# Three pieces of the gates' chain in the linear attention of an encoder block

## The chip, the core and the metric

The kernel runs on one core of one Trainium2 chip. The metric is the device time of one execution in microseconds (us). Three runs of the kernel before took 1631.79, 1632.20 and 1633.09 us; the median is 1632.2 us.

## The reference: what is computed

One layer of an encoder on 1024 tokens with 1024 features. After an RMS norm the input is multiplied by `w_in`, and the columns are split into the queries, keys and values of two attention branches and their gates. Branch A is a gated linear attention with 4 heads, run in both directions:

```python
b = jnp.cumsum(log_g, axis=3)
q_dec = q * jnp.exp(b)
k_inv = k * jnp.exp(-b)
scores = jnp.where(mask, jnp.einsum("bhncd,bhnmd->bhncm", q_dec, k_inv), 0.0)
...
def step(state, inp):
    kv_n, dec_n = inp
    return dec_n[..., None] * state + kv_n, state
...
o_inter = jnp.einsum("bhncd,nbhde->bhnce", q_dec, states)
```

Per chunk of tokens, `b` is the running sum of the log gates; the queries are scaled by exp(b), the keys by exp(-b), and a state (keys by values) goes from one chunk to the next. Branch B is an attention in a window of 128 tokens. Both are gated, added and projected, and a feed-forward part follows.

## The kernel before, in words

All matrix products are float32 products out of float32r parts: each operand is split into a high part, made by ScalarE (ACT), and a low part, made by VectorE (DVE) as the difference, and three matmuls high x high, high x low, low x high are added (`mm3`, lines 76 to 79). TensorE (PE) is handed its instructions in the order in which the program is written (`manual_schedule` for PE). For ACT, DVE and the queue of transfers (SP) a scheduler lays down the order when the program is built: of what it takes for ready it puts first what was written first. On the chip each engine then works through its list in order.

The part around the change is the linear attention: 4 heads with 8 chunks of 128 tokens each, in time slots `t` (lines 597 to 614). Chunks go in pairs. For head `hd` and an even chunk `c`, with n = 8 hd + c:

- `g_gates` (lines 395 to 443) at the head of slot n, an even slot: loads the pair's q and k (`qk`), multiplies the gate codes out (`z`), and makes the gates in one tile `G` (one buffer) by a chain that goes back and forth between ACT and DVE: exponential (L418, ACT), a cap (L419, DVE), logarithm (L420, ACT), running sum (L421, DVE), the chunk ends `sm` (L424, L425), the differences (L428, L429, DVE), two exponentials of `G` (L431 and L432, ACT), the products with k and q (`en` in L434, `G` in L435, DVE), and the splits `kh`, `kl` (L438, L439) and `q2f`, `q2b` (L442, L443).
- `g_scores` (L445) at slot n+3, an odd slot: loads and splits v (`vh`, `vl`), turns `en` round on PE (`kt`, split to `kth`, `ktl`), multiplies the scores, and makes the masked scores `sp` (L470 ACT, L471 DVE), `sh` (L474) and `sl` (L475), the last two on DVE.
- `g_out` (L480) for each chunk at slot n+4: the chunk's keys times values `kv` on PE; the new state `pf` on DVE (L489, or L493 for a head's first chunk); a copy `kb` of the other direction's part (L491, ACT); for the next chunk the decayed state, split to `th` (L501, ACT) and `tl` (L502, DVE); then the output `o` on PE from `sh`, `sl` and from the `th`, `tl` of the chunk before, and its copy `ob` (L509, ACT).
- `g_back_out` (L523) for the other direction, later: adds its product to `ob` (L531, DVE) and moves the backward state one chunk on (`thb` in L520, `tlb` in L521, `kb` in L523).
- `g_turn` (L546): turns a finished chunk round on PE and copies it (`ot`, L552, ACT).

The small products write to a pool of four PSUM banks (`ch`), so a new product waits until an older one's bank has been read by the copy or the addition named above. A second pool of four banks (`mm`) serves the dense projections.

`slot` (L267) writes the stages of a slot in a fixed order, gates, turns, `g_back_out`, `g_out`, `g_scores`, and after each stage an equal share of the slot's dense projection matmuls (34 a slot at first, later 21, 18 and 11, from `GF`). So `g_out` of an even slot comes behind the gates' stage, and that of the odd slot half a slot later comes near the slot's head. The dense matmuls read weights that `wunit` has split two units ahead (`wh` L67, `wl` L69); their results leave by `st` (L138, L141 on DVE, L220 on ACT). DVE also does passes over the input for a later stage (`xn`, L563 and L568).

Of the kernel before, what the change touches and what calls it, by code (L numbers as in the profile page):

```python
# [23 lines left out]
GF = ((8, 34), (24, 21), (36, 18), (1 << 30, 11))  # L24
# [6 lines left out]
def body(tc, i, out):  # L31
    nc = tc.nc
    with ExitStack() as root:
# [8 lines left out]
        def nm(s):  # L42
            uid[0] += 1
            return f"{s}_{uid[0]}"
# [4 lines left out]
        def chtile(shape, dt=F32):  # L49
            return psc.tile(list(shape), dt, tag="ch", name=nm("ch"))  # L50
# [21 lines left out]
        def mm(o, a, b, start, stop):  # L72
            nc.tensor.matmul(o, a, b, start=start, stop=stop)  # L73
# [40 lines left out]
        def put(key, t):  # L114
            d = scratch("_".join(map(str, key)))
            nc.sync.dma_start(out=d, in_=t)
            scr[key] = d
# [139 lines left out]
        def fill(n):  # L257

            while n > 0 and dense:
                try:  # L260
                    next(dense[0])
                    n -= 1
                except StopIteration:
                    dense.pop(0)

        def share(plan, t):
            return next(n for end, n in plan if t < end)  # L267

        def need(key):
            while key not in scr:  # L270
                fill(12)

        def slot(stages, n):

            stages = [f for f in stages if f]
            done = 0
            if not stages:
                fill(n)
            for j, f in enumerate(stages):
                f()  # L280
                t = n * (j + 1) // len(stages)
                fill(t - done)
                done = t
# [106 lines left out]
        def gtile(tag, shape=(P, 256), dt=F32, bufs=2):  # L390
            return gt.tile(list(shape), dt, tag=tag, name=nm(tag), bufs=bufs)
# [4 lines left out]
        gla = {}  # L396

        def g_gates(hd, c):


            pr = Chunk()
            for j in range(2):
                a = gla[hd, c + j] = Chunk()
                a.pr, a.j, a.t = pr, j, slice(j * P, (j + 1) * P)
            s, co = c // 4, (c % 4) * P
            for nme in ("q", "k"):
                need((f"{nme}{hd}", s))
            qk = gtile("qk", (P, 2, 256))
            nc.sync.dma_start(out=qk[:, 0], in_=scr[f"q{hd}", s][:, co:co + 256])
            nc.sync.dma_start(out=qk[:, 1], in_=scr[f"k{hd}", s][:, co:co + 256])  # L410
            z = chtile((P, 2, 256))
            for d in range(2):
                mm(z[:, d], upS[:, d, hd * P:(hd + 1) * P], lrS[:, c * P:(c + 2) * P], True, True)
            G = gtile("G", (P, 4, 2, P), bufs=1)
            Gt = G.rearrange("p a j t -> p a (j t)")
            Gf = G.rearrange("p a j t -> p (a j t)")
            cs, e, csf, ef = G[:, 0:2], G[:, 2:4], Gf[:, 0:512], Gf[:, 512:1024]
            nc.scalar.activation(ef, z.rearrange("p d t -> p (d t)"), AF.Exp, scale=-1.0)  # L418
            nc.vector.tensor_scalar(ef, ef, float(np.expm1(8.0)), None, op0=ALU.min)  # L419
            nc.scalar.activation(ef, ef, AF.Ln, bias=ones[:, 0:1])  # L420
            nc.vector.tensor_tensor_scan(csf, mask.rearrange("p c t -> p (c t)"), ef, 0.0, op0=ALU.mult, op1=ALU.add)  # L421

            pr.sm = gtile("sm", (P, 2, 2, 2), bufs=16)
            nc.vector.tensor_scalar(pr.sm, cs[:, :, :, 63:128:64], -1.0 / 16, None, op0=ALU.mult)  # L424
            nc.vector.tensor_tensor(pr.sm[:, :, :, 1], pr.sm[:, :, :, 1], pr.sm[:, :, :, 0], op=ALU.subtract)  # L425

            late = bass.AP(Gf.tensor, Gf.offset, [list(Gf.ap[0]), [255, 2], [P, 2], [1, P]])
            nc.vector.tensor_tensor(e, late, cs[:, :, :, 63:64].to_broadcast([P, 2, 2, P]), op=ALU.subtract)  # L428
            nc.vector.tensor_scalar(e[:, 1, :, 0:1], cs[:, 1, :, 63:64], -1.0, None, op0=ALU.mult)  # L429

            nc.scalar.activation(csf, ef, AF.Exp, scale=-1.0 / 16)  # L431
            nc.scalar.activation(ef, ef, AF.Exp, scale=1.0 / 16)  # L432
            pr.en = gtile("en", (P, 2, 256))
            nc.vector.tensor_tensor(pr.en, Gt[:, 1:3], qk[:, 1:2].to_broadcast([P, 2, 256]), op=ALU.mult)  # L434
            nc.vector.tensor_tensor(Gt[:, 0:4:3], Gt[:, 0:4:3], qk[:, 0:1].to_broadcast([P, 2, 256]), op=ALU.mult)  # L435
            pr.kh = gtile("kh", (P, 2, 256), FR)
            pr.kl = gtile("kl", (P, 2, 256), FR)
            nc.scalar.activation(pr.kh, pr.en, AF.Copy)  # L438
            nc.vector.tensor_tensor(pr.kl, pr.en, pr.kh.bitcast(F32), op=ALU.subtract)  # L439
            pr.q2 = (gtile("q2f", (P, 2, 256), FR, bufs=3), gtile(f"q2b{c}", (P, 2, 256), FR, bufs=(3, 2, 2, 1)[c // 2]))  # L440
            for q2, x in zip(pr.q2, (Gt[:, 0], Gt[:, 3])):
                nc.scalar.activation(q2[:, 0], x, AF.Copy)  # L442
                nc.vector.tensor_tensor(q2[:, 1], x, q2[:, 0].bitcast(F32), op=ALU.subtract)  # L443
# [116 lines left out]
        def x_norm(k, s):  # L560
            t = xn.tile([P, HT], F32, tag="xn", name=nm("xn"))
            nc.sync.dma_start(out=t, in_=i["xT"][k, s])
            tc.keep_in_program_order(nc.vector.scalar_tensor_tensor(  # L563
                t, t, g1[:, k:k + 1], rstd[:, s * HT:(s + 1) * HT], op0=ALU.mult, op1=ALU.mult))
            return t

        def x_diff(key, k, d, a, b):
            tc.keep_in_program_order(nc.vector.tensor_tensor(d, a, b, op=ALU.subtract))  # L568
            put((key, k), d)

        def x_sums():
            for k in range(KT // 2):
                a = x_norm(k, 0)
                yield
                b = x_norm(k, 1)
                yield
                x_diff("xT1", k, b, b, a)
                yield
                c = x_norm(k + 4, 1)
                put(("x22", k), c)  # L580
                yield
                x_diff("xT2", k, b, c, b)
                yield
                x_diff("xT3", k, a, b, a)
                yield
                c = x_norm(k + 4, 0)
                yield
                x_diff("xT4", k, c, c, b)
                yield
# [4 lines left out]
        qg = load_const(swk, "qg", i["qg"], (P, P))  # L594
        kg = load_const(swk, "kg", i["kg"], (P, P))

        at = {}
        last = 0
        for n in range(NH * NC):
            hd, c = divmod(n, NC)  # L600
            cb = hd * NC + NC + 4 + (NC - 1 - c)
            tt = cb + c % 2 + 2
            for j, (t, f) in enumerate(((n, g_gates), (n + 3, g_scores), (n + 4, g_out),
                                        (cb, g_back_out), (tt, g_turn))):
                if j > 1 or c % 2 == 0:
                    at[t, j + (j == 4 and c % 2)] = (f, hd, c)
                last = max(last, t)
        sums = x_sums()
        with tc.manual_schedule(engines={mybir.EngineType.PE}):
            fill(36)  # L610
            for t in range(last + 1):
                slot([(lambda v=at[t, j]: v[0](*v[1:])) if (t, j) in at else None for j in (0, 5, 4, 3, 2, 1)], share(GF, t))
                if t:
                    next(sums, None)
        glas.close()
# [185 lines left out]
        for n in range(2 * KT):  # L801
            t, g = divmod(n, 2)
# [101 lines left out]
        def pair_T3(f):  # L904
            nme, m, a, b = PAIRS[f]
            g = pend[f]
            product(g.X, wsplit(g.s3, 512), XT["T3"], 4, False, True)
            return result((f"{nme}{m + 4}", 1), g.X, g.p5)
# [69 lines left out]
        with tc.manual_schedule(engines={mybir.EngineType.PE}):  # L978
# [15 lines left out]
            for j in range(0, len(PAIRS), 2):  # L994
# [4 lines left out]
                v = [pair_T3(f) for f in two]  # L999
# [554 lines left out]
```

## Time and profile before

| what | value |
|---|---|
| median of three runs | 1632.2 us (1631.79 to 1633.09) |
| the profiled execution | 1632.87 us; its span, from the first to the last instruction, 1631.1 us |
| granted TensorE clock | 1.00 |
| PE, DVE, ACT busy in the span | 1614.8, 1228.7, 911.6 us |
| slots of the linear attention | from 48.5 us (first L418) to 373 us (last `ot`) |
| gates' chains | 16, the first scan (L421) at 50.95 us, the last at 307.08 us |

How to read it: a row of the timeline gives the start, the duration, the engine, the line, what is written and from what; in brackets stands the idle time of the engine just before and what ended it. Starts of neighbours on one engine lie closer together than durations, since they overlap at their ends. "PE" rows are matmuls, "PEld" the loading of their weights. The list of waits adds up such idle times by the instruction that ended them: total, number, longest.

### The profile page before, as it was taken

To read this page: it belongs to the slowest core of one execution; us is meant where nothing else is said; L and a number is where in the kernel's file an instruction comes from. 1 tells how busy PE (TensorE), PEld (TensorE's weight loads), DVE (VectorE), ACT (ScalarE), POOL (GpSimd) and SP (SyncE) were. 2 spreads that over 40 slices of the span, in tenths; PEclk is the share of its full clock that TensorE was granted. 3 is DMA by queue.
4 is the path that set the end of the run, shared out by engine and by line. 5 is a ranking of instruction groups with operands and counts; after the bars stand their busy time and mean duration, and the time that the engine had idled before them with its cause. 6 is when DMAs were issued, how large, how long until landed. Compare 5 with 4: busy or idle time off the path is not lost.

```text
span 1631.1 us, 23428 instructions
## 1 busy us (share of the span) xinstructions
PE 1614.8 (99%) x7644; PEld 1342.6 (82%) x7644; DVE 1228.7 (75%) x2358; ACT 911.6 (56%) x1867; POOL 0.2 (0%) x4
## 2 busy tenths in 40 slices
PE   9999999999999999999999999999999999999999
PEld 7888888788888888888888888888888888788887
DVE  8568888855989777876955888677777888779655
ACT  7456776873888854544733556754444444354442
POOL 0000000000000000000000000000000000000000
PEclk9999999999999999999999999999999999999999
DMA  8855847788553478777943566643435464695433
GB/s 279 299 171 191 255 152 265 265 268 291 184 165 107 133 253 265 258 239 263 296 123 103 167 201 214 205 142 112 148 111 182 166 221 146 201 331 190 149 97 117
DMA packets 196363, 323.26 MB, mean 198 GB/s; under 512 B 22318, under 2 KB 47790, under 8 KB 196240
## 3 DMA queue, kind: packets, MB, share of 16 engines
q1 hardware_dynamic: 196240, 321.76, 60.4%
q8 instruction: 60, 0.98, 0.3%
q14 instruction: 63, 0.52, 0.1%
HBM read 216.29 MB, written 105.38 MB: 197 GB/s over the span
## 4 chain that ended last, share of the span: by engine, by line
PE 88%; DVE 5%; ACT 4%; DMA 2%; issue 1%; SPq 0%; ACTq 0%; DVEq 0%
PE mm L73 19%; PE mm L856 10%; PE mm L858 10%; PE mm L857 10%; PE mm L1394 7%; PE ch L73 6%; PE ch L1394 6%; PE ch L856 5%; PE ch L858 5%; PE ch L857 5%; PE mm L245 3%; PE ch L762 1%; ACT p L745 1%; DVE G L421 1%; PE ch L712 0%
## 5 line engine op out<-in xcount | busy, mean ns | idle before, releaser
L835 ACT ACTIVATE wh<-ws 128x512 fp32r<-128x512 f32 x164 | 103.0, 630 | 154.1 <-PE mm L857 83.0
L73 PE MATMUL mm<-wh,xh 128*128 128x512 f32 x320 | 127.2, 398 | 1.1 <-ACT st L220 1.1
L73 PE MATMUL mm<-wh,xl 128*128 128x512 f32 x320 | 127.1, 397 | 0.0
L73 PE MATMUL mm<-wl,xh 128*128 128x512 f32 x320 | 126.6, 396 | 0.0
L836 DVE TENSOR_TENSOR wl<-ws,wh 128x512 fp32r<-128x512 f32 x164 | 112.1, 686 | 14.6 <-ACT wh L835 14.2
L67 ACT ACTIVATE wh<-wr 128x512 fp32r<-128x512 f32 x118 | 73.5, 627 | 55.1 <-PE mm L73 21.6
L69 DVE TENSOR_TENSOR wl<-wr,wh 128x512 fp32r<-128x512 f32 x118 | 80.7, 686 | 21.7 <-ACT wh L67 21.3
L835 ACT ACTIVATE wh<-a 128x512 fp32r<-128x512 f32 x66 | 41.7, 632 | 91.1 <-PE ch L1394 42.3
L835 ACT ACTIVATE wh<-wr 128x512 fp32r<-128x512 f32 x76 | 47.9, 631 | 58.9 <-PE mm L857 19.7
L836 DVE TENSOR_TENSOR wl<-a,wh 128x512 fp32r<-128x512 f32 x66 | 45.6, 690 | 41.0 <-ACT wh L835 40.6
L1394 PE MATMUL mm<-hh,wh 128*128 128x512 f32 x176 | 68.6, 390 | 0.6 <-DVE c L1333 0.6
L1394 PE MATMUL mm<-hl,wh 128*128 128x512 f32 x176 | 68.7, 390 | 0.0
L73 PEld LDWEIGHTS mm<-wh,xh 128*128 128x128 f32 x320 | 60.3, 188 | 10.3 <-ACT st L220 1.3
L1394 PE MATMUL mm<-hh,wl 128*128 128x512 f32 x176 | 68.5, 389 | 0.0
L73 PEld LDWEIGHTS mm<-wl,xh 128*128 128x128 f32 x320 | 60.2, 188 | 9.8
L73 PEld LDWEIGHTS mm<-wh,xl 128*128 128x128 f32 x320 | 60.2, 188 | 9.7
L849 DVE TENSOR_TENSOR ws<-wr,wr 128x512 f32<-128x512 f32 x80 | 54.5, 686 | 5.5 <-DMA wr<-in_w_oa_dram 2.5
L836 DVE TENSOR_TENSOR wl<-wr,wh 128x512 fp32r<-128x512 f32 x76 | 51.9, 685 | 7.7 <-ACT wh L835 7.1
L1367 DVE TENSOR_TENSOR hl<-hr,hh 128x512 fp32r<-128x512 f32 x77 | 52.8, 685 | 6.0 <-ACT hh L1366 6.0
L1366 ACT ACTIVATE hh<-hr 128x512 fp32r<-128x512 f32 x77 | 47.6, 618 | 8.9 <-DMA hr<-B 5.0
L1394 PE MATMUL ch<-hh,wh 128*128 128x512 f32 x132 | 51.3, 389 | 0.0
L1394 PE MATMUL ch<-hl,wh 128*128 128x512 f32 x132 | 51.3, 389 | 0.0
(454 smaller groups left out, 4987.1 us busy)
## 6 DMA issues: line engine op xcount, KB each, us to landing
wr<-in_w_fi_dram SPq DMA_DIRECT2D x110, 256.0 KB, 4.0
wr<-in_w_f_dram SPq DMA_DIRECT2D x100, 256.0 KB, 3.7
wh<-wh SPq DMA_DIRECT2D x80, 256.0 KB, 3.3
wl<-wl SPq DMA_DIRECT2D x80, 256.0 KB, 3.0
B<-c SPq DMA_DIRECT2D x44, 256.0 KB, 2.1
T<-st SPq DMA_DIRECT2D x44, 256.0 KB, 2.9
a<-in_w_fo_dram SPq DMA_DIRECT2D x44, 256.0 KB, 5.3
hr<-T SPq DMA_DIRECT2D x44, 256.0 KB, 2.6
```

The lines of the kernel that those rows point to most:

```text
L67: nc.scalar.activation(h, raw, AF.Copy)
L69: nc.vector.tensor_tensor(l, raw, h.bitcast(F32), op=ALU.subtract)
L73: nc.tensor.matmul(o, a, b, start=start, stop=stop)
L245: nc.tensor.matmul(Y[q], w[:, c], x, start=f0, stop=f1, skip_group_check=True)
L835: nc.scalar.activation(h, src, AF.Copy)
L836: nc.vector.tensor_tensor(l, src, h.bitcast(F32), op=ALU.subtract)
L849: nc.vector.tensor_tensor(t, x, y, op=op)
L856: nc.tensor.matmul(o, h[:, c], x[kk][0], start=start and kk == 0, stop=False, skip_group_check=True)
L857: nc.tensor.matmul(o, h[:, c], x[kk][1], start=False, stop=False, skip_group_check=True)
L858: nc.tensor.matmul(o, l[:, c], x[kk][0], start=False, stop=kk == nk - 1, skip_group_check=True)
L1367: nc.vector.tensor_tensor(l, r, h.bitcast(F32), op=ALU.subtract)
L1394: nc.tensor.matmul(ys[m], a[:, c], b, start=f0, stop=f1, skip_group_check=True)
```

## The change

`g_gates` is cut into three functions, called at three places. What stays in `g_gates`, at the head of slot n: the loads of `qk`, the matmuls `z`, and the chain up to the chunk ends `sm` (L425). `g_decays` is called in the same slot n, right behind its last stage (`g_out`, once there are outputs) and ahead of that stage's dense matmuls: the differences, the two exponentials and the products with k and q. `g_parts` is called in the odd slot n+1, right behind its last stage (`g_scores`): the splits `kh`, `kl`, `q2f`, `q2b`. No instruction is added or taken away, and none gets another shape; the matmuls on PE, and which dense matmuls stand between them, are the same ones in the same order. Tiles keep their numbers of buffers. In slots that had no stage before, the piece is the only stage and the dense matmuls follow it.

```diff
             nc.vector.tensor_tensor(pr.sm[:, :, :, 1], pr.sm[:, :, :, 1], pr.sm[:, :, :, 0], op=ALU.subtract)
 
+            pr.qk, pr.G = qk, G
+
+        def g_decays(hd, c):
+            pr = gla[hd, c].pr
+            qk, G = pr.qk, pr.G
+            Gt = G.rearrange("p a j t -> p a (j t)")
+            Gf = G.rearrange("p a j t -> p (a j t)")
+            cs, e, csf, ef = G[:, 0:2], G[:, 2:4], Gf[:, 0:512], Gf[:, 512:1024]
             late = bass.AP(Gf.tensor, Gf.offset, [list(Gf.ap[0]), [255, 2], [P, 2], [1, P]])
             nc.vector.tensor_tensor(e, late, cs[:, :, :, 63:64].to_broadcast([P, 2, 2, P]), op=ALU.subtract)
...
             nc.vector.tensor_tensor(Gt[:, 0:4:3], Gt[:, 0:4:3], qk[:, 0:1].to_broadcast([P, 2, 256]), op=ALU.mult)
+
+        def g_parts(hd, c):
+            pr = gla[hd, c].pr
+            Gt = pr.G.rearrange("p a j t -> p a (j t)")
             pr.kh = gtile("kh", (P, 2, 256), FR)
...
-        at = {}
+        at, behind = {}, {}
...
+            if c % 2 == 0:
+                behind[n] = (g_decays, hd, c)
+                behind[n + 1] = (g_parts, hd, c)
...
-                slot([(lambda v=at[t, j]: v[0](*v[1:])) if (t, j) in at else None for j in (0, 5, 4, 3, 2, 1)], share(GF, t))
+                work = [[at[t, j]] for j in (0, 5, 4, 3, 2, 1) if (t, j) in at]
+                if t in behind:
+                    work = work or [[]]
+                    work[-1].append(behind[t])
+                slot([lambda v=v: [f(*a) for f, *a in v] for v in work], share(GF, t))
```

What the scheduler made of it differs in the order of neighbours on ACT, DVE and SP. Below are three places; the lines of the changed kernel are 8 higher from L428 to L435 of before, 12 higher up to the slots, and 19 higher in the attention that follows them.

**Slot 8** (head 1's first pair of chunks; `pf`, `th`, `tl` belong to the output of head 0's chunk 4). On ACT before, from the copy of an output to `kh`:

```order
L509 COPY ob_253_1482<-ch_1475 128x256
L431 ACTIVATE G_1417<-G_1417 128x512
L491 COPY kb_248_1467<-ch_1458 128x256
L432 ACTIVATE G_1417<-G_1417 128x512
L501 ACTIVATE th_1471<-pf_1465,dec_1469 128x256
L498 ACTIVATE dec_1509<-sm_1191,sm_971 128x1
L438 ACTIVATE kh_1432<-en_1429 128x512
```

The same place on ACT in the changed kernel, where the two exponentials are L439 and L440:

```order
L521 COPY ob_248_1465<-ch_1458 128x256
L503 COPY kb_243_1450<-ch_1441 128x256
L513 ACTIVATE th_1454<-pf_1448,dec_1452 128x256
L439 ACTIVATE G_1417<-G_1417 128x512
L510 ACTIVATE dec_1499<-sm_1191,sm_971 128x1
L440 ACTIVATE G_1417<-G_1417 128x512
L450 ACTIVATE kh_1580<-en_1471 128x512
```

`kb` and `th` have moved ahead of the two exponentials. On DVE before:

```order
L489 SCALAR_TENSOR_TENSOR pf_1465<-pf_1303,dec_1307,ch_1458 128x256
L429 TENSOR_SCALAR G_1417<-G_1417 128x2
L434 TENSOR_TENSOR en_1429<-G_1417,qk_1411 128x512
L435 TENSOR_TENSOR G_1417<-G_1417,qk_1411 128x2x256
L502 SCALAR_TENSOR_TENSOR tl_1472<-pf_1465,dec_1469,th_1471 128x256
L439 TENSOR_TENSOR kl_1433<-en_1429,kh_1432 128x512
```

And on DVE in the changed kernel:

```order
L501 SCALAR_TENSOR_TENSOR pf_1448<-pf_1293,dec_1297,ch_1441 128x256
L437 TENSOR_SCALAR G_1417<-G_1417 128x2
L514 SCALAR_TENSOR_TENSOR tl_1455<-pf_1448,dec_1452,th_1454 128x256
L442 TENSOR_TENSOR en_1471<-G_1417,qk_1411 128x512
L443 TENSOR_TENSOR G_1417<-G_1417,qk_1411 128x2x256
L580 TENSOR_TENSOR xn_1408<-xn_1408,xn_854 128x512
```

`tl` has moved ahead of the two products, and `kl` has gone further back.

**Slot 20** (the third pair of head 2). On ACT before, from the logarithm to the copy of a turned chunk, with two results of a projection (`st`) between:

```order
L420 ACTIVATE G_2765<-G_2765,ones 128x512
L220 ACTIVATE st_2815<-mm_2326,rstdt 128x512
L67 ACTIVATE wh_2988<-wr_2986 128x512
L501 ACTIVATE th_2833<-pf_2829,dec_2831 128x256
L431 ACTIVATE G_2765<-G_2765 128x512
L220 ACTIVATE st_2846<-mm_2327,rstdt 128x512
L432 ACTIVATE G_2765<-G_2765 128x512
L552 COPY ot_2870<-ch_2867 128x256
```

In the changed kernel:

```order
L420 ACTIVATE G_2765<-G_2765,ones 128x512
L220 ACTIVATE st_2798<-mm_2309,rstdt 128x512
L67 ACTIVATE wh_2988<-wr_2986 128x512
L220 ACTIVATE st_2836<-mm_2310,rstdt 128x512
L513 ACTIVATE th_2816<-pf_2812,dec_2814 128x256
L439 ACTIVATE G_2765<-G_2765 128x512
L564 COPY ot_2860<-ch_2857 128x256
L440 ACTIVATE G_2765<-G_2765 128x512
```

The second `st` has moved ahead of `th`, and `ot` ahead of the second exponential.

**Slots 22 and 23** (the end of head 2's gates). On DVE before, from `tl` to the addition `ob` of the other direction:

```order
L502 SCALAR_TENSOR_TENSOR tl_3071<-pf_3064,dec_3068,th_3070 128x256
L439 TENSOR_TENSOR kl_3019<-en_3015,kh_3018 128x512
L443 TENSOR_TENSOR q2f_3022<-G_3003,q2f_3022 128x256
L443 TENSOR_TENSOR q2b_646_3023<-G_3003,q2b_646_3023 128x256
L568 TENSOR_TENSOR xn_2526<-xn_2625,xn_2526 128x512
L138 SCALAR_TENSOR_TENSOR st_3102<-mm_2849,rstd 128x512
L138 SCALAR_TENSOR_TENSOR st_3106<-mm_2850,rstd 128x512
L531 TENSOR_TENSOR ob_478_2381<-ob_478_2381,ch_3135 128x256
```

In the changed kernel:

```order
L514 SCALAR_TENSOR_TENSOR tl_3054<-pf_3047,dec_3051,th_3053 128x256
L580 TENSOR_TENSOR xn_2526<-xn_2615,xn_2526 128x512
L138 SCALAR_TENSOR_TENSOR st_3092<-mm_2839,rstd 128x512
L138 SCALAR_TENSOR_TENSOR st_3096<-mm_2840,rstd 128x512
L451 TENSOR_TENSOR kl_3220<-en_3070,kh_3219 128x512
L543 TENSOR_TENSOR ob_473_2364<-ob_473_2364,ch_3125 128x256
L455 TENSOR_TENSOR q2f_3223<-G_3003,q2f_3223 128x256
L455 TENSOR_TENSOR q2b_697_3224<-G_3003,q2b_697_3224 128x256
```

The pass over the input, the two results `st` and the addition `ob` have moved ahead of the splits `q2f` and `q2b`.

## The prediction

> **What bounds the kernel now.** I read the page's busy times first, then PE's waits in the linear attention, then four windows, then the timeline around the waits. The page's first part:
>
> ```profile
> PE 1614.8 (99%) x7644; PEld 1342.6 (82%) x7644; DVE 1228.7 (75%) x2358; ACT 911.6 (56%) x1867; POOL 0.2 (0%) x4
> ```
>
> PE is busy in 99% of the span. The change puts nothing else on PE and leaves PE's order alone, so it can win only time in which PE waits, and only where the change reaches: the slots, from 45 to 345 us. PE's waits there, all of them (total, number, longest):
>
> ```profile
> PE ch L73 <- DVE tl L502: 1.6, 3, 0.9
> PE ch L73 <- ACT ot L552: 1.1, 2, 0.9
> PE mm L73 <- ACT st L220: 1.1, 1, 1.1
> PE ch L73 <- DVE ob L531: 0.6, 2, 0.4
> PE ch L73 <- ACT th L501: 0.3, 1, 0.3
> PE ch L73 <- DVE sl L475: 0.3, 1, 0.3
> PE ch L73 <- DVE sh L474: 0.3, 1, 0.3
> ```
>
> That is 5.3 us in 11 waits. Three windows hold them; the window 250 to 278 has none. Columns: busy time of PE, PEld, DVE, ACT and POOL, the granted clock, the DMA share, GB/s:
>
> ```profile
> 125.00:151.00 26.00, 24.42 (x143) 20.98 (x142) 22.01 (x48) 16.48 (x41) 0.00 (x0) 1.00 0.57 183
> 222.00:250.00 28.00, 26.48 (x154) 22.01 (x153) 23.98 (x58) 21.07 (x60) 0.00 (x0) 1.00 0.56 187
> 250.00:278.00 28.00, 28.00 (x159) 24.21 (x158) 22.51 (x50) 16.43 (x45) 0.00 (x0) 1.00 0.85 282
> 278.00:322.00 44.00, 41.78 (x246) 35.36 (x245) 38.95 (x92) 36.96 (x104) 0.00 (x0) 1.00 0.74 247
> ```
>
> PE's gaps are 1.58, 1.52 and 2.22, 5.3 again, at a clock of 1.00 everywhere. But a wait costs more than its bracket. Two of them on PE's timeline:
>
> ```profile
> 144.22 0.28 PE L73 MATMUL ch<-vl,sh 128*128 128x256 f32 x1
> 144.34 0.28 PE L73 MATMUL ch<-vh,sl 128*128 128x256 f32 x1
> 144.95 0.39 PE L73 MATMUL ch<-th,q2f 128*128 128x256 f32 x1 [0.34 <-ACT th L501]
> 146.28 0.38 PE L73 MATMUL ch<-tl,q2f 128*128 128x256 f32 x1 [0.94 <-DVE tl L502]
> ```
>
> Undisturbed neighbours start 0.12 apart (144.22, 144.34); here the steps are 0.61 and 1.33, so 0.49 + 1.21 = 1.70 is lost where the brackets say 1.28: 0.21 more for each restart. Eleven waits make the pool 5.3 + 11 x 0.21 = 7.6 us. That is all the change can remove.
>
> The Trainium skill (Perfetto Trace Analysis, Identifying the Most-Contended Engine) says that matmul busy time is a poor measure of PE's headroom, since pipelined matmuls look smaller, and that the busy share of LDWEIGHTS is a good one. By that rule the three windows, held against the quiet one, miss 98 x 24.21/28.00 - 78.35 = 6.4 us of loading, or 7.4 us of time. The trace agrees: the starts give 7.6, the busy time 5.3. By the busy time alone the sum below would be about -2.5.
>
> **The change part by part.** *The second piece, L428 to L435, behind the outputs.* Slot 8 on ACT and DVE:
>
> ```profile
> 126.70 0.63 ACT L431 ACTIVATE G<-G 128x512 f32<-128x512 f32 x1 [0.42 <-DVE G L429]
> 127.24 0.35 ACT L491 COPY kb<-ch 128x256 f32<-128x256 f32 x1
> 127.49 0.63 ACT L432 ACTIVATE G<-G 128x512 f32<-128x512 f32 x1
> 128.03 0.50 ACT L501 ACTIVATE th<-pf,dec 128x256 fp32r<-128x256 f32 x1
> ```
>
> ```profile
> 128.16 0.69 DVE L434 TENSOR_TENSOR en<-G,qk 128x512 f32<-128x512 f32 x1 [1.55 <-ACT G L432]
> 128.77 0.68 DVE L435 TENSOR_TENSOR G<-G,qk 128x512 f32<-128x512 f32 x1
> 129.37 0.48 DVE L502 SCALAR_TENSOR_TENSOR tl<-pf,dec,th 128x256 fp32r<-128x256 f32 x1
> ```
>
> In the changed order `th` stands ahead of both exponentials, 0.54 + 0.54 = 1.08 us of ACT (starts 126.70 to 127.24 and 127.49 to 128.03), and `tl` ahead of `en` and `G`, 129.37 - 128.16 = 1.21 of DVE. DVE's wait of 1.55 for the exponential no longer lies ahead of `tl` either. The waits on record for `th` and `tl` are 0.3 (one) and 1.6 (three), all behind an even slot's gates. (a) **All four go: 1.9 + 4 x 0.21 = 2.7.** The largest, 0.49 + 1.21, is covered because both steps come forward there.
>
> *Outputs that wait in ACT's row.* Slot 20 on ACT:
>
> ```profile
> 223.82 0.62 ACT L431 ACTIVATE G<-G 128x512 f32<-128x512 f32 x1
> 224.34 0.67 ACT L220 ACTIVATE st<-mm,rstdt 128x512 f32<-128x512 f32 x1
> 224.91 0.62 ACT L432 ACTIVATE G<-G 128x512 f32<-128x512 f32 x1
> 225.43 0.36 ACT L552 COPY ot<-ch 128x256 f32<-128x256 f32 x1
> ```
>
> PE waited 0.9 for this `ot`; the exponential that `ot` passes is worth 225.43 - 224.91 = 0.52; the second `st` and `th` still stand ahead of it. Of the pool's `ot` 1.1, `st` 1.1 and `ob` 0.6 (2.8 in five waits, 3.9 with restarts) I take about half: 0.7 of `ot`, 0.3 of `st`, since its bank waits behind a full row, and all 0.6 of `ob` with its restarts, 0.4. (b) **2.0 go**, with bounds of 0 and 3.9.
>
> *The third piece, L438 to L443, a slot later.* Slots 22 and 23 on DVE:
>
> ```profile
> 242.45 0.68 DVE L439 TENSOR_TENSOR kl<-en,kh 128x512 fp32r<-128x512 f32 x1
> 243.05 0.42 DVE L443 TENSOR_TENSOR q2f<-G,q2f 128x256 fp32r<-128x256 f32 x1
> 243.38 0.42 DVE L443 TENSOR_TENSOR q2b<-G,q2b 128x256 fp32r<-128x256 f32 x1
> 243.72 0.69 DVE L568 TENSOR_TENSOR xn<-xn,xn 128x512 f32<-128x512 f32 x1
> 244.32 1.28 DVE L138 SCALAR_TENSOR_TENSOR st<-mm,rstd 128x512 f32<-128x512 f32 x2
> 245.52 0.41 DVE L531 TENSOR_TENSOR ob<-ob,ch 128x256 f32<-128x256 f32 x1
> ```
>
> The three splits hold DVE from 242.45 to 243.72, 1.27 us. `q2f` and `q2b` now come behind `ob`, 0.67 of it, more than the longest `ob` wait of 0.4: that is why I let `ob` go. `kl`, `q2f` and `q2b` themselves are read from slot n+3 on, over a slot after their new place, so their lateness costs PE nothing; without that cover it would be their 1.27 a pair. `G` has one buffer, so the next pair's first exponential must wait for `q2b`; between the two lies the rest of an odd slot.
>
> (c) The waits for `sh` and `sl` (0.6, 1.0 with restarts) stay: both stand on DVE ahead of the third piece's new place, and nothing ahead of them is taken away.
>
> (d) **What comes in their place: 1.1.** Work that was ready early now fills the holes: the order puts passes `xn` (0.69 each) ahead of `sl` in some odd slots, and one `sl` has a slack of only 0.24 (rows in the last rival). 0.69 - 0.24 + 0.21 = 0.66 there at most, 0 if DVE was idle before it; I take 0.6, near the upper end, since DVE's row nearest to it (242.45 to 245.52 above) has no gap. And in 278 to 322 DVE works 38.95 of 44.00, so PE, coming earlier, meets it late once more: 0.5, between 0 and the 2.2 that the window loses now.
>
> No wait is added. `th`, which waits for `pf`, now stands ahead of the exponentials on ACT, so those, `en` and `G` wait behind it; PE reads what becomes of them three slots on. SP's loads of `qk` stay at the slot's head, and none of PE's waits above was for a transfer.
>
> Sum: -2.7 - 2.0 + 1.1 = **-3.6**. Against the profiled execution, 1632.87, that is 1629.3; it lies 0.7 above the median, 1632.2, from which it gives **1628.6**.
>
> **The rivals.** *Everything goes.* PE's eleven waits are all of one kind, something late by up to 1.2 us, and the pieces free 1.08 on ACT and 1.21 + 1.27 on DVE per pair. Then -7.6: 1624.6. Against it: `sh` and `sl` are passed by nothing. Chance 0.13.
>
> *Given back.* In the last window DVE is 89% busy, and in 222 to 250 it is 86%. If DVE's own work sets the pace there, only the burst at 125 to 151 is won, 0.46 + 1.70 = 2.2 with its three restarts (the first is the 0.3 for `tl` that is left of the 1.6 and 0.3), less 1.0 of new waits as in (d): 1631.0. Chance 0.17.
>
> *Too few banks.* The waits for `ot`, `ob` and `st` are for four `ch` and four `mm` banks in rotation; if they only move along, (a) alone is won, less (d): -1.6, 1630.6. The Trainium skill (Perfetto Trace Analysis, Optimization Strategy) says that consistent bubbles can mean too little SBUF or PSUM for the next tile; here five of eleven waits are of that kind, but not in a steady beat, which speaks against it. Chance 0.11.
>
> *Slower: the pieces fall ahead of the scores.* `en` and `G` (1.21) and the splits (1.27) now compete in DVE's row with `sh` and `sl`, which come in the odd slots, where the gates had been done long before. Two `sl` on DVE, and their readers on PE with a third place:
>
> ```profile
> 218.78 0.42 DVE L475 TENSOR_TENSOR sl<-sp,sh 128x256 fp32r<-128x256 f32 x1
> 235.06 0.42 DVE L475 TENSOR_TENSOR sl<-sp,sh 128x256 fp32r<-128x256 f32 x1
> ```
>
> ```profile
> 219.44 0.28 PE L73 MATMUL ch<-vh,sl 128*128 128x256 f32 x1
> 236.51 0.28 PE L73 MATMUL ch<-vh,sl 128*128 128x256 f32 x1
> 320.63 0.28 PE L73 MATMUL ch<-vl,sh 128*128 128x256 f32 x1
> 320.96 0.39 PE L73 MATMUL ch<-vh,sl 128*128 128x256 f32 x1
> ```
>
> Slacks: 219.44 - 219.20 = 0.24, 236.51 - 235.48 = 1.03, none at 320.96 (a step of 0.33 where 0.12 is usual), and none where the 0.3 for `sl` is on record. A delay d costs 4d - 1.27 + 2 x 0.21 there. With both pieces, d = 2.48, that is 9.1; against the 4.7 of (a) and (b) the kernel loses 4.4: 1636.6. It is slower than before from d = 1.4, by over 0.2% from d = 2.2. For it: little slack. Against it: in the order the splits are written behind the scores, and the scheduler takes what was written first. Chance 0.15.
>
> **How the numbers follow.** The forecast has 0.44, with a range of its own from 1627.0 ((d) nothing, (b) a little more) to 1630.3 ((b) 0.3). 0.2% is 3.3 us, about what a measurement of this kernel can tell from no change: 1628.9. Of the forecast 0.30 lies below, 0.14 above. Faster: 0.30 + 0.13 + 0.02 from the middle cases = 0.45; same: 0.14 + 0.26 = 0.40; slower: 0.15. The range reaches from 1624.6 to 1633.5, where (d) takes its upper bounds, 0.66 + 2.2, against the 2.2 of the first burst alone (1632.9), and half the spread of the three runs, (1633.09 - 1631.79) / 2 = 0.65, is added; outside lie the slower case and a little below.
>
> **What would show it.** Right: PE's list of waits has no `th` or `tl` any more, `ob` gone, `ot` and `st` shorter, `sh` and `sl` still there and perhaps longer; PE's gaps in the windows 125 to 151 and 222 to 250 under 0.5 us each. Wrong: new waits for `sl`, `sh` or `ktl` in odd slots of a us or more, waits for `kl` or `q2f`, a DVE over 95% busy around 278 to 322, or a difference that arises outside 45 to 345 us.

## The result and the profile after

The changed kernel takes 1629.11 us (median of 11 runs, 1627.65 to 1631.99); the kernel before, run beside it, 1632.95 us (11 runs, 1631.32 to 1634.92). The ratio is 0.9978, with a 95% interval of 0.9971 to 0.9986: 3.6 us less, between 2.3 and 4.7. The forecast was 3.6 less. As a sum it held; of its four terms (d) was far too small, and what the other terms and some uncounted small hold-ups gave beyond the forecast made up for it.

PE's waits of the changed kernel from 45 to 345 us (total, number, longest; L141, L220, L564 and L486 are `st` on DVE, `st` on ACT, `ot` and `sh`):

```profile
PE mm L73 <- DVE st L141: 1.8, 1, 1.8
PE mm L73 <- ACT st L220: 1.0, 1, 1.0
PE ch L73 <- ACT ot L564: 0.2, 1, 0.2
PE ch L73 <- DVE sh L486: 0.2, 1, 0.2
```

The waits for `th`, `tl` and `ob` are gone, and of those for `ot` only 0.2 is left. But the longest wait of the list is a new one, for a result `st` on DVE, and the old one for an `st` on ACT has hardly changed. The windows of before, and one more:

```profile
125.00:151.00 26.00, 25.22 (x147) 21.69 (x145) 22.51 (x49) 16.47 (x42) 0.00 (x0) 1.00 0.53 177
152.00:156.00 4.00, 3.96 (x12) 3.19 (x13) 3.18 (x7) 1.71 (x3) 0.00 (x0) 0.59 0.70 266
222.00:250.00 28.00, 28.00 (x167) 24.36 (x166) 24.86 (x61) 21.57 (x61) 0.00 (x0) 1.00 0.58 191
278.00:322.00 44.00, 42.45 (x253) 36.36 (x252) 39.52 (x94) 36.44 (x104) 0.00 (x0) 1.00 0.79 263
```

From 222 to 250 PE no longer waits at all. The 0.78 that is missing from 125 to 151 is the first part of one wait, which ends at 152. In the 4 us from 152 on, the granted clock is 0.59. Here is that place on PE:

```profile
149.60 0.39 PE L73 MATMUL mm<-wl,xh 128*128 128x512 f32 x1
149.82 0.40 PE L73 MATMUL mm<-wh,xl 128*128 128x512 f32 x1
152.04 0.50 PE L73 MATMUL mm<-wh,xh 128*128 128x512 f32 x1 [1.82 <-DVE st L141]
152.38 0.40 PE L73 MATMUL mm<-wl,xh 128*128 128x512 f32 x1
...
153.36 0.63 PE L73 MATMUL mm<-wh,xh 128*128 128x512 f32 x1
153.79 0.63 PE L73 MATMUL mm<-wl,xh 128*128 128x512 f32 x1
```

The step across the wait is 2.22 where 0.23 is usual, so 1.99 is lost; then steps of 0.43 follow until 156.

Since PE's matmuls come in the same order in both kernels, the start of one and the same matmul in the two traces tells how far ahead the changed kernel is. Four matmuls serve as marks; they start at 48.03, 168.02, 252.20 and 346.14 in the kernel before, and at 47.69, 168.95, 250.40 and 342.83 in the changed one. So the changed kernel is 0.34 ahead at the first mark, 0.93 behind at the second, 1.80 ahead at the third and 3.31 at the last. By stretches: **1.27 lost in the first, 2.73 won in the second, 1.51 won in the third**, 2.97 won in all. The 0.34 at the start and some 1.3 after the last mark lie outside the stretch from 45 to 345; they differ from one execution to the next (0.24 and 0.4 in e1 below, which is the same kernel). The same marks are used for every experiment.

### The profile page after: what moved, and what is told of

Its sections match the earlier page's. It is cut to its first block, busy times and chain, and to the rows that moved or that the text cites. A ratio compares the mean times of both kernels' runs of the same rounds, so it can differ in the third digit from the quotient of the medians.

```text
span 1626.5 us, 23425 instructions
## 1 busy us (share of the span) xinstructions
PE 1613.5 (99%) x7644; PEld 1343.2 (83%) x7644; DVE 1227.7 (75%) x2358; ACT 911.5 (56%) x1867; POOL 0.2 (0%) x4
## 4 chain that ended last, share of the span: by engine, by line
PE 90%; DVE 4%; ACT 4%; DMA 2%; issue 1%; SPq 0%; ACTq 0%; DVEq 0%
PE mm L73 19%; PE mm L875 10%; PE mm L877 10%; PE mm L876 10%; PE mm L1413 7%; PE ch L73 7%; PE ch L1413 6%; PE ch L876 5%; PE ch L875 5%; PE ch L877 5%; PE mm L245 3%; PE ch L781 1%; ACT p L764 1%; ACT xh L323 1%; ACT sq L330 0%
```

## The experiments

Theory A, from the prediction: the gain is the state parts `th` and `tl` coming ahead of the exponentials and products (second piece). Rival B: the third piece brings it, by freeing DVE. About the loss in the first stretch, theory A says that the time won at 130 and 146 was given back at 152, where DVE's row sets when `st` comes; rival C says that DVE sets the pace all over this stretch, so that any wait taken away comes back nearby.

**e1, the changed kernel again.** No edit.

> The changed kernel once more, as a yardstick for the others. If the new wait of 1.8 us for the output st (L141) at 152 us comes from the order on DVE, it stands in this profile too, between 1.7 and 1.9; if it was an accident of one execution, it is gone or under 1. The lower granted clock behind it (0.59 from 152 to 156) may come or not: if the wait alone sets it off it comes again. Ratio to before 0.9970 to 0.9986.

Ratio 0.9979 (0.9970 to 0.9988). The wait for `st` is there again (1.9), the marks give +1.40, -2.70 and -1.52 (minus is won). The pattern belongs to the program.

**e2, the second piece alone; e3, the third piece alone.** In e2 both lines of the table `behind` become one, and the slot appends both functions; in e3 the second piece goes back to the slot's head:

```diff
-                behind[n] = (g_decays, hd, c)
-                behind[n + 1] = (g_parts, hd, c)
+                behind[n] = ((g_decays, hd, c), (g_parts, hd, c))     # e2
+                at[n, 0] = (lambda *v: (g_gates(*v), g_decays(*v)), hd, c)     # e3
+                behind[n + 1] = (g_parts, hd, c)                               # e3
```

> Only the second piece moved (L428 to L435 of before behind the outputs); the splits follow it directly. Theory A (the gain is the state parts th and tl coming ahead of the exponentials and products): the waits for th and tl are gone, the ob waits (0.6) stay because the splits again stand ahead of ob, and the wait for st at 152 stays: 2 to 3 us faster than before, ratio 0.9980 to 0.9990. Rival B (the third piece frees DVE and brings the gain): within 1 us of before, waits for tl still 1 us or more.

> Only the third piece moved (the splits kh, kl, q2f, q2b into the odd slot); the exponentials and products stay at the slot's head. Theory A: the waits for th and tl stay (1.5 to 2 us), those for ob go (0.6 and their restarts, 1.0), no wait for st at 152, since PE does not come earlier there: 0.5 to 1.5 us faster, ratio 0.9990 to 0.9997. Rival B: 3 us or more faster.

e2: ratio 1.0003 (0.9994 to 1.0011); marks -0.24, -0.50, -0.36. e3: ratio 0.9978 (0.9969 to 0.9988); marks -0.56, -1.93, -1.56, in all 4.05 won. PE's waits in e2 and then in e3 (lists of waits from 45 to 345):

```profile
PE mm L73 <- DVE st L141: 1.9, 1, 1.9
PE ch L73 <- DVE sh L486: 1.2, 2, 0.9
PE ch L73 <- DVE ob L543: 1.1, 2, 0.6
PE mm L73 <- ACT st L220: 0.4, 1, 0.4
PE ch L73 <- ACT ob L521: 0.3, 1, 0.3
PE ch L73 <- DVE sl L487: 0.3, 2, 0.2
```

```profile
PE mm L73 <- ACT st L220: 1.7, 1, 1.7
PE ch L73 <- DVE tl L514: 1.0, 2, 0.6
PE ch L73 <- ACT ob L521: 0.4, 1, 0.4
```

In the lists each piece does to its own waits roughly what theory A said: the second takes all for `th` and `tl` and leaves 1.1 for `ob` on DVE (at 230 and 314, though, where the kernel before had 229 and 246); the third takes those for `ob` on DVE and leaves 1.0 for `tl`, less than the 1.5 to 2 expected, and none for `th`. But their worth is the other way round. The second piece gives back at 152 what it won, and the third alone is as fast as both. Theory A falls as an account of where the time went; B holds for the total. That freed time on DVE is how the third piece does it, these two runs do not show.

**e4, more room at 152.** The `st` of 152 us and a second one right behind it on DVE each free one of the four `mm` banks for the next projection (v1, first half), whose first unit goes through its four tiles in turn, three matmuls each. e4 takes the first two units by pairs of tiles, so PE has 12 matmuls to do ahead of the freed banks instead of 6:

```diff
                         us.append(next_unit())
-                        if k < KT - 2:
+                        if (name, s) == ("v1", 0) and k < 2:
+                            if k:
+                                for t2 in (0, 2):
+                                    for k2 in range(2):
+                                        for t in (t2, t2 + 1):
+                                            yield from unit_mm(k2, t)
+                        elif k < KT - 2:
                             for t in range(4):
                                 yield from unit_mm(k, t)
```

> The changed kernel, with the first two units of one projection (v1, first half) taken by pairs of banks, so that PE needs the two banks that the st of 152 us frees 6 matmuls (1.4 us) later. Theory A (the 2.2 us won at 130 and 146 are given back at 152, where DVE's closed row sets when st comes): the wait there falls from 1.8 to under 0.5 and PE is 1.4 to 2 us ahead of the changed kernel behind it, up to 3.5 where the clock also stays at 1.00: ratio to before 0.9960 to 0.9970. Rival C (DVE sets the pace in all of this stretch): as much wait turns up at the next places within 20 us, and the ratio stays near 0.9978.

Ratio 0.9971 (0.9960 to 0.9983); 1627.67 us (6 runs) where e1, on the same chip, took 1629.2. (Part of this is the clock: 5 of e1's 11 executions show a mean clock below 1.000, none of e4's.) No wait at 152, the clock at 1.00, and marks of -2.25, -1.44 and -1.52: 5.21 won. `st` on DVE in e4, and PE's 12th and 13th matmul of the projection:

```profile
150.78 0.68 DVE L141 TENSOR_TENSOR st<-mm,rstd 128x512 f32<-128x512 f32 x1
```

```profile
151.39 0.40 PE L73 MATMUL mm<-wh,xl 128*128 128x512 f32 x1
151.63 0.40 PE L73 MATMUL mm<-wh,xh 128*128 128x512 f32 x1
```

`st` ends at 151.46, only 0.17 ahead of the 13th matmul. In the first stretch C is refuted: what was won is kept. In the second it has a point, since 1.3 less is won there than by the changed kernel.

**e5, fewer steps ahead of `st`.** Updates `kb` of the backward state stood in DVE's row ahead of `st`, two of them written later in the program than that `st`:

```diff
-                    nc.vector.scalar_tensor_tensor(a.kb, n.kb, dec[:, 0:1], a.kb, op0=ALU.mult, op1=ALU.add)
+                    tc.keep_in_program_order(nc.vector.scalar_tensor_tensor(a.kb, n.kb, dec[:, 0:1], a.kb, op0=ALU.mult, op1=ALU.add))
```

> The changed kernel, with each update of the backward state kb (L523 of before) kept behind what was written before it on DVE. In the row ahead of the st at 152 two of the four kb (149.99 to 151.0) drop out; the step ktl ahead of them cannot come earlier, since it waits for kth on ACT until 149.4. If DVE's closed row sets when st comes, st starts about 1.0 earlier and PE's wait falls from 1.8 to between 0.5 and 1.1; ratio to before 0.9970 to 0.9978. If DVE is simply too slow for this whole stretch, the kb updates are missed later and as much wait turns up within 20 us.

Ratio 0.9975 (0.9965 to 0.9985), marks -0.79, -2.47, -1.25. The changed kernel's DVE row up to `st`:

```profile
147.44 0.48 DVE L533 SCALAR_TENSOR_TENSOR tlb<-kb,decb,thb 128x256 fp32r<-128x256 f32 x1
147.84 1.00 DVE L535 SCALAR_TENSOR_TENSOR kb<-kb,decb,kb 128x256 f32<-128x256 f32 x2
148.90 0.48 DVE L533 SCALAR_TENSOR_TENSOR tlb<-kb,decb,thb 128x256 fp32r<-128x256 f32 x1
149.38 0.69 DVE L475 TENSOR_TENSOR ktl<-ch,kth 128x512 fp32r<-128x512 f32 x1
149.99 1.06 DVE L535 SCALAR_TENSOR_TENSOR kb<-kb,decb,kb 128x256 f32<-128x256 f32 x2
150.97 0.43 DVE L483 COPY_PREDICATED sp<-tri,ch 128x256 f32<-128x256 uint32 x1
151.30 0.68 DVE L141 TENSOR_TENSOR st<-mm,rstd 128x512 f32<-128x512 f32 x1
```

And e5's:

```profile
148.23 0.48 DVE L535 SCALAR_TENSOR_TENSOR kb<-kb,decb,kb 128x256 f32<-128x256 f32 x1
149.29 0.48 DVE L533 SCALAR_TENSOR_TENSOR tlb<-kb,decb,thb 128x256 fp32r<-128x256 f32 x1 [0.58 <-ACT thb L532]
149.69 0.48 DVE L535 SCALAR_TENSOR_TENSOR kb<-kb,decb,kb 128x256 f32<-128x256 f32 x1
150.09 0.68 DVE L475 TENSOR_TENSOR ktl<-ch,kth 128x512 fp32r<-128x512 f32 x1
150.85 0.45 DVE L483 COPY_PREDICATED sp<-tri,ch 128x256 f32<-128x256 uint32 x1
151.19 0.68 DVE L141 TENSOR_TENSOR st<-mm,rstd 128x512 f32<-128x512 f32 x1
```

The wait fell from 1.8 to 1.3; 0.5 to 1.1 was expected to be left. Seen from the first mark (0.38 later in this execution), `st` comes 0.49 earlier: two `kb` are out of the row, but `tlb` now waits 0.58 for `thb` on ACT and holds the row. So `st`'s time is set by what stands ahead of it on DVE, waits included. Within the next 20 us no new wait turned up; one of 0.65 for `sh` is new at 316.

**e6, the kernel before with such a bank order; e7, the changed kernel with it; e8, the third piece alone with it.** The condition of e4 is widened to all these projections but v0:

```diff
-                        if (name, s) == ("v1", 0) and k < 2:
+                        if name != "v0" and k < 2:
```

> The kernel before, with the first two units of each such projection (all but v0) taken by pairs of banks. If the bank order only gives room where PE comes too early, the kernel before gains little by it: no wait at 153 was there, the st wait at 295 (1.05, with its restart 1.2) goes, those for th, tl, ob and ot stay: 0.5 to 1.5 us faster, ratio 0.9990 to 0.9997. If the bank order is a gain by itself, 3 us or more, ratio under 0.9982.

> The changed kernel with the same bank order in all these projections. Both st waits (1.8 at 152, 1.0 at 293) fall under 0.3: 2.5 to 4 us less than the changed kernel in the slots, ratio to before 0.9955 to 0.9968. If the waits only move on, the ratio is that of the run with one projection reordered, 0.9971, or worse.

> As e7, with the third piece alone moved. If the second piece is worth the waits for tl and th at 130 and 146 and this was hidden only by the wait at 152, this kernel shows those waits again (1.0 and restarts) and is 1 to 2 us slower than e7. If the third piece alone brings the gain, it is within 0.5 us of e7.

e6: 0.9993 (0.9984 to 1.0002), marks -0.84, -0.40, -0.02. e7: 0.9967 (0.9955 to 0.9980), marks -1.65, -1.41, -2.05. e8: 0.9967 (0.9955 to 0.9980), marks -1.12, -1.90, -2.30. The bank order is little by itself. In e7 the `st` wait at 293 is gone, but a wait of 1.1 for the output copy `ob`, on ACT as well, stands at 292 in its place (in e6 too, 1.2), and by the marks e7, 5.11 ahead in all, is no further than e4 with one projection reordered. The second piece adds nothing to the third here: e7 is 0.5 ahead of e8 in the first stretch and loses it in the second; by time they lie within the 0.5 us that had been set for this, though e8 still has 0.7 of waits for `tl`.

**e9, one reason for the end of the `ot` wait.** In the kernel before, a pass over the input (`xn`, 0.68) stood on DVE between `sl` and the cap of the next gates' chain (L419):

```profile
219.12 0.68 DVE L568 TENSOR_TENSOR xn<-xn,xn 128x512 f32<-128x512 f32 x1
219.72 0.42 DVE L419 TENSOR_SCALAR G<-G 128x512 f32<-128x512 f32 x1
```

In the changed kernel and in e3 the cap stands right behind `sl`, at 219.20 and 219.11, and the chain came sooner. e9 moves that pass, and the one of slot 27, in the kernel before:

```diff
+                if t in (19, 27):
+                    next(sums, None)
                 slot([(lambda v=at[t, j]: v[0](*v[1:])) if (t, j) in at else None for j in (0, 5, 4, 3, 2, 1)], share(GF, t))
-                if t:
+                if t and t not in (19, 27):
                     next(sums, None)
```

> The kernel before, with the passes over the input of slots 19 and 27 written ahead of the slot's stages instead of behind them, so that on DVE no pass (0.68) stands between sl and the cap of the next gates' chain at 219. Theory E: what the third piece won at 226 is this pass, which went forward into the room that the splits left. Then the chain on ACT and DVE comes 0.6 earlier, ot with it, and PE's wait for ot (0.9) falls under 0.4; the waits for ob at 229 and 246 and those for tl and th stay: 0.5 to 1 us faster in the slots, ratio 0.9993 to 0.9999. Rival: the room on ACT (kh, q2f, q2b) brings ot forward; then the wait for ot stays at 0.7 or more.

Ratio 0.9998 (0.9989 to 1.0007), marks -0.22, -0.81, +0.28. PE's first waits in the second stretch:

```profile
224.83 0.38 PE L73 MATMUL ch<-vh,kth 128*128 128x256 f32 x1 [0.45 <-ACT ot L552]
226.78 0.39 PE L73 MATMUL ch<-vh,sh 128*128 128x256 f32 x1 [0.98 <-ACT ob L509]
```

The wait for `ot` halves, from 0.89 to 0.45, between the two expectations. But the output's copy `ob` now waits on ACT behind `q2f` and `q2b`:

```profile
225.76 0.40 ACT L442 ACTIVATE q2f<-G 128x256 fp32r<-128x256 f32 x1
226.07 0.40 ACT L442 ACTIVATE q2b<-G 128x256 fp32r<-128x256 f32 x1
226.38 0.35 ACT L509 COPY ob<-ch 128x256 f32<-128x256 f32 x1
```

So the pass explains about half of the `ot` wait, and what it wins is lost again at once behind the splits on ACT; in e3, where the splits are out of the way too, the wait for `ot` is gone and that for `ob` on ACT is 0.37. The 0.81 of this stretch comes later, from 240 to 246: there the `ob` wait of 0.44 goes, against the expectation, although the splits still stand ahead of that `ob` on DVE. DVE's chain comes 1.5 earlier there, seen from the first mark.

**e10, a wait that was to be longer.** As e4, but with the other pair of tiles first:

```diff
-                                for t2 in (0, 2):
+                                for t2 in (2, 0):
```

> The changed kernel, with the first two units of the projection v1 (first half) begun with the two banks that the st of 152 us frees, so that PE needs them 6 matmuls (1.4 us) earlier. If DVE's row sets when st comes, st stands at the same time as in the changed kernel (about 151.3) and PE's wait grows from 1.8 to 3.2; PE is 1.4 us later behind it. If a long wait is what brings the lower granted clock, it comes here for certain (under 0.65 in the 4 us behind the wait). Ratio to before 0.9980 to 0.9996. If PE's own coming sets st's time, the wait stays near 1.8.

No wait came at 152; ratio 0.9971 (0.9960 to 0.9982), marks -2.31, -1.42, -1.55, as in e4. `st` starts at 150.92, and PE does the projection's first 12 matmuls from 148.78 on without a wait; so the pair that is now first has the free banks. The program appears to give the banks out in order of first use, and the edit did not make what it was meant to. It serves as a second run of e4 and tells nothing on longer waits.

**e11, the second piece alone with e4's bank order; e12, the third alone with it.** The edits are those of e2 and e3 above, each on top of e4's.

> The second piece alone, with the one projection (v1, first half) started by pairs of banks as in e4. If the second piece is worth the waits for th and tl at 130 and 146 as soon as there is room at 152, PE keeps 2.0 to 2.4 us of the first burst, and the slots give about 3 us in all: ratio to before 0.9980 to 0.9987. If the second piece is worth nothing even with that room, the ratio is 0.9993 to 1.0003, and the waits turn up elsewhere.

> The third piece alone, with the same one projection started by pairs of banks. Its own wait at 152 was only 0.2, so the bank order should bring it under 0.4 us: ratio 0.9970 to 0.9978, with the waits for tl (1.0 and restarts) still there, and 1 us slower than e4 if the second piece is worth those waits; the same as e4 (0.9971) and no wait for tl if it is worth nothing.

e11: 0.9982 (0.9973 to 0.9991), marks -2.41, -0.28, -0.36. e12: 0.9973 (0.9963 to 0.9983), marks -1.16, -1.88, -1.58. With room at 152 the second piece keeps its 2.4 us of the first stretch, which it had lost in e2. On top of the third piece it is worth 1.1 there (e4 against e12, 2.25 and 1.16), less 0.4 in the second stretch; by the times, 0.9971 and 0.9973, the two cannot be told apart.

The marks by piece, with minus for won:

| kernel | 48 to 168 | 168 to 252 | 252 to 346 | sum | ratio |
|---|---|---|---|---|---|
| changed | +1.27 | -2.73 | -1.51 | -2.97 | 0.9978 |
| e2, second piece | -0.24 | -0.50 | -0.36 | -1.10 | 1.0003 |
| e3, third piece | -0.56 | -1.93 | -1.56 | -4.05 | 0.9978 |
| e11, second, room at 152 | -2.41 | -0.28 | -0.36 | -3.05 | 0.9982 |
| e12, third, room at 152 | -1.16 | -1.88 | -1.58 | -4.62 | 0.9973 |
| e4, both, room at 152 | -2.25 | -1.44 | -1.52 | -5.21 | 0.9971 |

e4, e7, e8, e10 and e12 took 1627.1 to 1627.7 us and are below both the kernel before and, by about 1.5 us, the changed one (on the same chip in e4 alone); which of them is best cannot be told apart.

## Why the prediction was right, and which of its steps were not

- **The pool** (7.6 us, and nothing outside the slots): held. The most that any kernel here wins in the slots is 5.3 (e8).
- **(a), `th` and `tl` go, 2.7:** the waits went, and the size was right: 2.41 of it, in the first stretch, is what e11 keeps. But in the changed kernel nothing of these 2.41 is left, because of (d); only the `tl` wait at 313, 0.6 with its restart, stays won.
- **(b), half of 3.9:** the total, 2.0, is about what came (`ot` 1.4 to 0.4 and `ob` 1.1 to nothing with restarts, `st` unchanged: 2.1). For `ob` the step named, the splits moved behind it, is enough, since both waits go in e3; it is not the only way, since the wait at 246 falls to 0.10 in e2 and to nothing in e9 with the splits still ahead. For `ot` the step named failed: passing the exponential was not needed, since e3 loses the wait with both exponentials still ahead of `ot`; a pass `xn` that went forward is half of it (e9). ACT in e3:

```profile
224.13 0.62 ACT L440 ACTIVATE G<-G 128x512 f32<-128x512 f32 x1
224.65 0.67 ACT L220 ACTIVATE st<-mm,rstdt 128x512 f32<-128x512 f32 x1
225.22 0.36 ACT L564 COPY ot<-ch 128x256 f32<-128x256 f32 x1
```

For `st` at 295 the reason given, "its bank waits behind a full row", was wrong: the row was not full. ACT in the kernel before, where that `st` follows at 295.10, and then in the changed kernel:

```profile
293.65 0.63 ACT L431 ACTIVATE G<-G 128x512 f32<-128x512 f32 x1 [1.60 <-DVE G L429]
```

```profile
291.39 0.51 ACT L513 ACTIVATE th<-pf,dec 128x256 fp32r<-128x256 f32 x1 [1.41 <-DVE pf L505]
291.80 0.62 ACT L439 ACTIVATE G<-G 128x512 f32<-128x512 f32 x1
292.32 0.67 ACT L220 ACTIVATE st<-mm,rstdt 128x512 f32<-128x512 f32 x1
```

ACT stood idle for 1.60 while the exponential at its head waited for `G` from DVE; now it stands idle for 1.41 while `th` waits for `pf`, and `st` is queued behind in both. The prediction had named this queue ("`th`, which waits for `pf`, now stands ahead") but only for the exponentials.

- **(c), `sh` and `sl` stay:** mostly held. By the steps between matmuls 0.9 was lost to them before and 0.6 is left, 0.3 for `sl` at its old place and 0.35 for `sh` at 317.
- **(d), 1.1 given back in odd slots and in 278 to 322:** this step failed, in place and in size. Where it was put, hardly anything came: the gaps in 278 to 322 fell from 2.22 to 1.55. Instead 1.99 came at 152, for a tile of which the prediction does not speak, and 1.7 more behind it. The trace of before had shown the place. The end of that `st` and the first matmul into its bank, in the kernel before:

```profile
151.84 0.68 DVE L141 TENSOR_TENSOR st<-mm,rstd 128x512 f32<-128x512 f32 x1
```

```profile
152.79 0.39 PE L73 MATMUL mm<-wh,xh 128*128 128x512 f32 x1
```

`st` ended at 152.52, 0.27 ahead of its reader, behind a DVE row without a gap from 146. In the changed kernel PE's matmul just ahead of it starts at 149.82 instead of 152.56, 2.74 earlier, and `st` ends at 151.98, 0.54 earlier; 2.74 - 0.54 - 0.27 = 1.93, and 1.99 came. From the trace of before alone, the 2.2 that the prediction itself won at 125 to 151, less the slack of 0.27, gives 1.9 for a `st` that stays where it is: that could have been priced. The 1.7 lost behind the wait is 0.1 at the restart and the rest the lower clock in this execution; nothing in the trace of before showed that.

- **The rivals:** "Everything goes" did not come; 3.2 us of waits are left. "Given back" said that the first burst is kept and the later windows lose; it was the reverse. "Too few banks" did not come for `ot` and `ob`, which went, but the new wait at 152 is one for a bank. The slower rival did not come: no wait for `sl` or `sh` over 0.2, none for `kl` or `q2f`. In e2, where the splits stay in the even slot, the longest wait for `sh` is 0.9.

That the total came out as forecast is in part luck. Added up by steps from the first mark to the last, the profiled execution wins 3.0 by (a), 2.3 by (b), 0.2 by (c) and 1.1 by small hold-ups that carry no bracket or a very short one and stood in no term (0.3 of it behind `thb` at 241); it loses 3.7 at 152, where (d) had 1.1. So (d) was 2.6 short, and the others together gave 1.9 more than forecast; nothing in the prediction ties the one to the other. Profile and time agree to within 1 us: 2.97 by the marks, 3.6 and 3.4 (e1) by the ratios. Why e2 is no faster by time, though it is 1.10 ahead by the marks, is in part the clock: in its profiled execution 1.9 is lost around 411, outside the slots, in a stretch with the low clock (below), and 8 of its 11 executions show a mean clock below 1.000, against 4 of 27 of the kernel before on the same chip. Whether that is all of it stays open.

## What to carry to other kernels

When a wait is taken away from a saturated engine, look in the old trace for the slack of everything that this engine reads next: whatever has less slack than the time won, and does not move forward itself, can become the next wait (here 0.27 of slack, 2.4 won, a wait of 1.82). Price each moved piece with that give-back, and test the pieces apart; here the piece with the plain argument was worth nothing until the next place had room, and the other brought the gain. Where such a place is a handover of banks, the order in which the following work takes its banks can give the room, here at no cost that shows (e6, 0.9993).

## What the hardware showed beside

The granted clock falls behind waits of PE of less than 2 us, and not each time. These are 4 to 5 us behind a wait: the first row e1 (one wait of 1.92), then e2 (one of 1.88), e2 again (two, 0.82 and 0.97, within 2.3 us) and e5 (two, 0.68 and 0.97):

```profile
152.20:157.00 4.80, 4.76 (x15) 3.81 (x16) 4.46 (x8) 1.84 (x3) 0.00 (x0) 0.64 0.76 288
```

```profile
153.00:157.00 4.00, 3.79 (x18) 3.18 (x19) 3.82 (x9) 1.95 (x3) 0.00 (x0) 1.00 0.73 277
414.00:418.00 4.00, 4.00 (x17) 3.49 (x16) 2.50 (x13) 1.98 (x9) 0.00 (x0) 0.57 0.59 199
```

```profile
409.00:413.00 4.00, 3.87 (x14) 3.34 (x14) 2.65 (x10) 2.21 (x9) 0.00 (x0) 0.57 0.80 270
```

These windows are wider than the low stretch. Within it (152.80 to 156.10 in the changed kernel, 414.30 to 417.60 in e2, 409.70 to 412.90 in e5) the clock is 0.50, and from 156.20 on in the changed kernel it is 1.00 again: the low stretch lasts some 3.4 us. A 512-column matmul then starts every 0.43 instead of 0.23, which costs about 1.6 us in the changed kernel, nearly as much as the wait. With 1.44 of such idle time (0.47 and 0.97, the kernel before at 411) the clock stayed at 1.00, with 1.66 in one wait (e3 and e9) too; with 1.58 in two (0.61 and 0.97, e3 at 411) it fell. Of the changed kernel's 11 executions three show a mean clock below 1.000. The Trainium skill (TensorE: Matmul & The Clock Gate, Part 1) describes two states of the clock, half and full, set by how busy PE was in a window of about 3.4 us that runs freely. The two states agree with these rows, and so does an element of chance, which such a window brings; that it takes a whole idle window for the clock to fall, as the section's table reads, does not, since 1.6 to 1.9 us of idle time were enough here. What length decides was not tried, as e10 did not make the longer wait.
